# Feed-forward pairs of a two-block transformer layer: a pair's up result evacuated in two parts inside the next pair, one weight sum moved behind a plain unit, a group's last activation turned at once

## The chip, the cores and the metric

One Trainium2 chip, one core. The metric is the device time of one execution in microseconds. The kernel before took 2154.33 us (median of three runs, 2153.94 to 2155.76).

The engines are named as in the profile: PE (TensorE, matrix products; PEld is its loading of the stationary operand), DVE (VectorE), ACT (ScalarE), POOL (GpSimd) and SP (SyncE, which issues the large loads).

## The reference, cut to what matters

Two blocks run one after the other on 256 tokens of width 2048, in float32: an attention layer with four kinds of attention, and a mixer layer. The change touches only the feed-forward part of the second block:

```python
y = _rms(h, norm_ffn_g[i])                                   # 256 x 2048
h = h + (jax.nn.silu(y @ w_gate[i]) * (y @ w_up[i])) @ w_down[i]
```

`w_gate` and `w_up` are 2048 x 5632, `w_down` is 5632 x 2048.

## The kernel before, in words

**Products.** Every float32 operand is split into a rounded part `hi` and a remainder `lo`, and each product is made of three matmuls (x_hi w_lo, x_hi w_hi, x_lo w_hi). A weight tile of 512 rows by 512 columns (1 MB, `raw`) is loaded by SP, cast to `hi` by ACT (L292) and subtracted to `lo` by DVE (L293).

**Units.** The whole program is a list of units, each with one weight tile (`run_units`, L258). At step j the kernel issues, in this order: the sums that stand before unit j (`plus(u.before)`, L277, DVE), its hi (ACT), its lo (DVE), the sums behind it (`plus(u.after)`), then the products and evacuation of unit q = j - 2 (`fn`), then one step of the first waiting task (`pump`), then the loads whose buffer has come free (`fetch`). Three hi and lo buffers rotate, so hi of unit j needs PE to be done with unit j - 3. All engines work through their instructions in the order of issue.

**A plain unit** has 24 matmuls: four 128-row slices of the weight, two halves of the tokens, three matmuls each.

**Pairs.** The 5632 columns are taken in 11 blocks of 512, in groups of 4, 4 and 3. A block's gate and up tiles make a pair (`pair_units`, L304), but for the first block of all, which is computed plainly. For the first 1024 of the 2048 rows the pair takes the two halves of the tokens, two halves of the rows and the two weights as a 2 x 2 by 2 x 2 block product and makes it with seven products in place of eight, from sums of weight tiles and prepared sums of the activations (`forms`). Each of the seven is a form unit of 12 matmuls: u1, u5, u6, u3, u7, u4, u2. The other 1024 rows are plain units: left0 and left1 (the code's `left`, gate) and right0 and right1 (`right`, up). Four accumulators of PE are used: a and b end as gate, c and d as up. Their banks come in turn from five.

- u5 leaves its product in c, and ACT copies it to the tile `sn` (`keep`, L328, "s5"); u6 adds to b, and ACT keeps minus b in `sn` ("s2"); u7 adds to b, and ACT copies minus b into the bank of d (L353). Then left0 adds first to a (12 matmuls) and then to b (12 matmuls).
- The sums on weight tiles are b11 += b12 ahead of u5, b11 += b22 behind u5's lo, b12 += b22 ahead of u6, and b11 += b21 behind u7's lo. The last makes what u4 reads.
- u2 ends gate; ACT writes its Silu into two tiles `sg` (L1436).
- right1 ends up: `up_evac` (L1438) adds the kept `sn` to c and to d (L1446), then multiplies by the row scale and by `sg` into the tile `act` (L1449), all on DVE, and adds a task that turns `act` (`late_turn`, L393: four empty steps, one more in `turn_gen`, then eight transposes on PE, L431, and two copies each on ACT, L447, and DVE, L448, into `xB`).

**The order around the change** (`weave`, L382): the last two units of what came before, here called right0 and right1 of the previous pair, stand among the first units of the next:

```
right0(prev) u1 right1(prev) u5 u6 u3 u7 left0 u4 left1 u2 right0 u1(next) right1 ...
```

In groups 1 and 2 the two units ahead of the first pair are the last two of the down product before. Behind a group's last pair come the units of the down product (`down_evac`, L1456): four column tiles, each over all blocks of the group; the unit that reads block i calls `need(("act", g, i))`, which finishes that block's turn there and then if it isn't done.

Of the kernel before, what the change touches and what calls it, by code (L numbers as in the profile page):

```python
# [9 lines left out]
F32 = mybir.dt.float32  # L10
F32R = mybir.dt.float32r
AF = mybir.ActivationFunctionType
ALU = mybir.AluOpType
# [4 lines left out]
P = 128  # L18
# [6 lines left out]
CH = 512  # L25
# [133 lines left out]
class Kernel:  # L159
# [144 lines left out]
    def pair_units(self, wl, wr, lhs, forms, evac_l, evac_r, need=None):  # L304

        nc = self.nc  # L310
        src = lambda w, r: w[r].rearrange("p (k n) -> p k n", n=CH)
        st = {}
        b11, b12, b21, b22 = (Load(src(w, r), 4, CH) for r in range(2) for w in (wl, wr))

        def product(key, x, hi, lo, first):
            xh, xl = x
            for k in range(4):
                for i, (x_, w_) in enumerate(((xh, lo), (xh, hi), (xl, hi))):
                    nc.tensor.matmul(  # L319
                        st[key], x_[:, k, :], w_[:, k, :], start=first and k + i == 0, stop=k == 3 and i == 2, skip_group_check=True  # L320
                    )

        def bank(key):
            st[key] = self.psM.tile([P, CH], F32, tag="mm", name="mm")

        def keep(key, src, scale):
            st[key] = self.p5.tile([P, CH], F32, tag="sn", name="sn", bufs=2)
            nc.scalar.activation(out=st[key], in_=st[src], func=AF.Copy, scale=scale)  # L328

        def block(r, m):  # L330
            return [x[:, 4 * r : 4 * r + 4, m * P : m * P + P] for x in lhs()]

        def p1(hi, lo):
            if need is not None:
                self.need(need)
            bank("a")
            bank("b")
            product("a", block(0, 0), hi, lo, True)
            nc.scalar.copy(out=st["b"], in_=st["a"])

        def p5(hi, lo):
            bank("c")
            product("c", forms()["F5"], hi, lo, True)
            keep("s5", "c", 1.0)

        def p6(hi, lo):
            product("b", forms()["F6"], hi, lo, False)
            keep("s2", "b", -1.0)

        def p7(hi, lo):  # L350
            product("b", forms()["F7"], hi, lo, False)
            bank("d")
            nc.scalar.activation(out=st["d"], in_=st["b"], func=AF.Copy, scale=-1.0)  # L353

        def p2(hi, lo):
            product("a", block(1, 0), hi, lo, False)
            evac_l((st["a"], st["b"]))

        def rest(w, r, keys, then=None):
            def fn(hi, lo):  # L360
                for m, key in enumerate(keys):
                    product(key, block(r, m), hi, lo, False)
                if then is not None:
                    then()

            return Unit(src(w, r), 4, CH, fn)

        form = lambda load, fn: Unit(None, 4, CH, fn, load)
        u1 = form(b11, p1)
        u5, u6, u3, u7 = form(b11, p5), form(b11, p6), form(b22, lambda hi, lo: product("c", forms()["F3"], hi, lo, False)), form(b12, p7)  # L370
        u4 = form(b11, lambda hi, lo: product("b", block(1, 1), hi, lo, False))
        u2 = form(b21, p2)
        left = [rest(wl, r, "ab") for r in (2, 3)]
        right = [rest(wr, 2, "cd"), rest(wr, 3, "cd", lambda: evac_r(st["c"], st["d"], st["s2"], st["s5"]))]
        u1.loads = [b11]
        u5.before, u5.loads = [(b11, b12)], [b12]
        u5.after, u5.loads = [(b11, b22)], [b12, b22]
        u6.before = [(b12, b22)]
        u7.after, u7.loads = [(b11, b21)], [b21]
        return [u1, u5, u6, u3, u7, left[0], u4, left[1], u2], right  # L380

    def weave(self, pairs):  # L382

        tail = [self.units.pop() for _ in range(2)][::-1]
        for head, right in pairs:
            u5 = head[1]
            tail[1].before, u5.before = u5.before, []
            tail[1].loads, u5.loads = tail[1].loads + u5.loads[:1], u5.loads[1:]
            self.units += [tail[0], head[0], tail[1]] + head[1:]
            tail = right  # L390
        self.units += tail

    def late_turn(self, *args):  # L393
        for _ in range(4):
            yield
        yield from self.turn_gen(*args)

    def forms_of(self, lhs, out):

        nc = self.nc  # L400
        hi, lo = lhs
        f = self.p5.tile([P, 4, 2, 4, P], F32R, tag="forms", name="forms")
        for n, key in enumerate(("F5", "F6", "F3", "F7")):
            out[key] = (f[:, n, 0], f[:, n, 1])
        for k in (0, 2):
            x = []
            for r in range(2):
                t = self.p5.tile([P, CH], F32, tag="sg", name="fx", bufs=2).rearrange("p (k t) -> p k t", k=2)
                ks = slice(4 * r + k, 4 * r + k + 2)
                nc.vector.tensor_tensor(out=t, in0=hi[:, ks, :].bitcast(F32), in1=lo[:, ks, :].bitcast(F32), op=ALU.add)  # L410
                x.append(t)
            s = [self.p5.tile([P, CH], F32, tag="sn", name="fs", bufs=2).rearrange("p (f k t) -> p f k t", f=2, k=2) for _ in range(2)]
            s5, s6, s3, s7 = s[0][:, 0], s[0][:, 1], s[1][:, 0], s[1][:, 1]
            a11, a21, a12, a22 = x[0][:, :, 0:P], x[0][:, :, P:T], x[1][:, :, 0:P], x[1][:, :, P:T]
            sub = lambda o, p, q: nc.vector.tensor_tensor(out=o, in0=p, in1=q, op=ALU.subtract)
            sub(s5, a21, a22)
            sub(s7, a11, a21)
            sub(s6, s5, a11)
            nc.vector.tensor_tensor(out=s3, in0=s6, in1=a12, op=ALU.add)
            for src, key in ((s5, "F5"), (s7, "F7"), (s6, "F6"), (s3, "F3")):  # L420
                h, l = (y[:, k : k + 2, :] for y in out[key])
                nc.scalar.copy(out=h, in_=src)
                nc.vector.tensor_tensor(out=l, in0=src, in1=h.bitcast(F32), op=ALU.subtract)
            yield
# [1001 lines left out]
    def ffn_units(self):  # L1426
        nc, a = self.nc, self.a
        kx = [(k, k) for k in range(KD)]
        wg, wu, wd = a["t_w_gate_2"], a["t_w_up_2"], a["t_w_down_2"]
        r3 = lambda m: self.rs[:, 6 + m : 7 + m]  # L1430
        sg, forms = {}, {}
# [3 lines left out]
                s = sg[m] = self.p5.tile([P, CH], F32, tag="sg", name="sg", bufs=2)  # L1435
                nc.scalar.activation(out=s, in_=ps[m], func=AF.Silu, scale=r3(m))  # L1436

        def up_evac(g, i):  # L1438
            def evac(*ps):
                t = self.p5.tile([P, 2, CH], F32, tag="act", name="act", bufs=1)  # L1440
                if len(ps) == 1:
                    ps = ps[0]
                else:
                    *ps, s2, s5 = ps
                    for m, s in enumerate((s2, s5)):
                        nc.vector.tensor_tensor(out=s, in0=ps[m], in1=s, op=ALU.add)  # L1446
                    ps = s2, s5
                for m in range(2):
                    nc.vector.scalar_tensor_tensor(out=t[:, m, :], in0=ps[m], scalar=r3(m), in1=sg[m], op0=ALU.mult, op1=ALU.mult)  # L1449
                if i == 0:  # L1450
                    self.actT = self.new_B()
                self.add(self.late_turn(lambda m: t[:, m, :], 4 * i, lambda: self.actT), name=("act", g, i))

            return evac

        def down_evac(g, c):  # L1456
            def evac(ps):
# [18 lines left out]
        for g, n in enumerate((4, 4, 3)):  # L1476
            lhs, pairs = lambda: self.yT2, []
            for i in range(n):
                if g == 0 and i == 0:
                    def fresh():  # L1480
                        self.to_ffn()
                        self.add(self.forms_of(self.yT2, forms), name="forms")

                    self.wide = [self.gemm(wg[0], kx, lhs, gate_evac, fresh=fresh, need=lambda gi: ("h2", gi))[0]]
                    self.gemm(wu[0], kx, lhs, up_evac(0, 0))
                else:
                    need = "forms" if g == 0 and i == 1 else None
                    pairs.append(self.pair_units(wg[c0 + i], wu[c0 + i], lhs, lambda: forms, gate_evac, up_evac(g, i), need))
            self.weave(pairs)
            kts = [(c0 * 4 + k, k) for k in range(4 * n)]  # L1490
            for c in range(4):
                tail = g == 2 and c == 0
                us = self.gemm(wd[c], kts, lambda: self.actT, down_evac(g, c), fresh=self.to_tail if tail else None, need=lambda gi, g=g: ("act", g, gi))
                if tail:
                    self.wide.append(us[0])
            c0 += n
# [116 lines left out]
```

## Time and profile before

| | us |
|---|---|
| median of three runs | 2154.33 |
| the profiled execution | 2153.68 |
| its span, first to last instruction | 2151.9 |
| PE busy | 2100.4 |
| DVE busy | 1325.9 |
| ACT busy | 989.8 |

The feed-forward stage runs from about 1310 to 2060 us of the span. The mean granted clock of PE over the span is 0.994 of full speed. A row of the trace gives its start and its length in us; "x2" joins neighbours of one kind; a bracket at the end is the engine's idle time ahead of the row and what is taken to have ended it. Where an instruction waits for several things, the profile names the one that came last by its record.

### The profile page before, as it was taken

Reading aid. Unit: us, or ns where it says so; the run is one execution under the profiler, and the core shown is the slowest. Engines: PE = TensorE matmul, PEld = TensorE weight load, DVE = VectorE, ACT = ScalarE, POOL = GpSimd, SP = SyncE. Lnnn points to the kernel's source line nnn. Section 1 sums busy time; section 2 is a strip of 40 time slices with the busy share of each in tenths; the row PEclk is TensorE's granted clock in tenths of the full one; section 3 lists DMA queues with packets and bytes.
Section 4 is the critical chain, followed back from the end, with each engine's and each line's share of the span. In section 5 each row is a group of like instructions: output and inputs, shape, how many; then the busy total and the mean of one; then the engine's idle time right before and its main releaser. Section 6 shows DMA issues by size and latency. Waiting matters only on the chain.

```text
span 2151.9 us, 22847 instructions
## 1 busy us (share of the span) xinstructions
PE 2100.4 (98%) x9472; PEld 1727.2 (80%) x9472; DVE 1325.9 (62%) x1110; ACT 989.8 (46%) x932; POOL 36.9 (2%) x65
## 2 busy tenths in 40 slices
PE   8999999999999999999999999999999999999998
PEld 6888888888888888888888888777877778777886
DVE  6457555544455555556599458874588744885554
ACT  5444444444344434445453545553355533554544
POOL 1100000000000000001000000000000000000000
PEclk9999999999999999999999999999999999999999
DMA  7744354455555555555655455555445554445453
GB/s 261 258 154 176 132 182 159 174 196 182 192 194 195 182 191 194 187 223 197 234 176 177 175 176 208 206 195 185 164 158 206 203 196 169 164 184 193 166 176 127
DMA packets 59128, 401.68 MB, mean 187 GB/s; under 512 B 6788, under 2 KB 7440, under 8 KB 12304
## 3 DMA queue, kind: packets, MB, share of 16 engines
q1 hardware_dynamic: 56592, 388.69, 50.3%
q0 software_dynamic: 2288, 11.43, 1.7%
q8 instruction: 74, 1.21, 0.2%
q14 instruction: 30, 0.25, 0.0%
q10 hardware_dynamic: 144, 0.11, 0.0%
HBM read 398.08 MB, written 4.47 MB: 187 GB/s over the span
## 4 chain that ended last, share of the span: by engine, by line
PE 87%; DVE 9%; issue 2%; ACT 1%; DMA 1%; SPq 0%; ACTq 0%; POOLq 0%; POOL 0%; DVEq 0%
PE mm L233 24%; PE mm L235 24%; PE mm L234 24%; PE mm L319 11%; DVE lo L293 5%; DVE raw L277 2%; PE at L431 2%; ACT hi L292 1%; DMA raw<-in_t_w_in_dram 1%; PE at L646 0%; DVE sn L1446 0%; PE at L988 0%; DVE act L1449 0%; PE at L638 0%; PE at L682 0%
## 5 line engine op out<-in xcount | busy, mean ns | idle before, releaser
L293 DVE TENSOR_TENSOR lo<-raw,hi 128x2048 fp32r<-128x2048 f32 (+3 forms) x405 | 906.6, 2247 | 608.8 <-ACT hi L292 608.6
L292 ACT CAST hi<-raw 128x2048 fp32r<-128x2048 f32 (+3 forms) x405 | 756.4, 1873 | 663.2 <-PE mm L235 473.8
L233 PE MATMUL mm<-lo,xA 128*128 128x512 f32 x1536 | 606.9, 395 | 7.1 <-DVE lo L293 6.2
L235 PE MATMUL mm<-hi,xA 128*128 128x512 f32 x1536 | 600.6, 391 | 0.0
L234 PE MATMUL mm<-hi,xA 128*128 128x512 f32 x1536 | 600.4, 391 | 0.0
L233 PEld LDWEIGHTS mm<-lo,xA 128*128 128x128 f32 x1536 | 289.8, 189 | 69.2 <-DVE lo L293 7.1
L235 PEld LDWEIGHTS mm<-hi,xA 128*128 128x128 f32 x1536 | 289.9, 189 | 61.1
L234 PEld LDWEIGHTS mm<-hi,xA 128*128 128x128 f32 x1536 | 290.0, 189 | 59.4
L319 PE MATMUL mm<-hi,xA 128*128 128x512 f32 x880 | 271.3, 389 | 0.0
L233 PE MATMUL mm<-lo,xB 128*128 128x512 f32 x608 | 242.7, 399 | 4.8 <-ACT xB L447 4.8
L235 PE MATMUL mm<-hi,xB 128*128 128x512 f32 x608 | 240.6, 396 | 5.1 <-DVE xB L448 5.1
L234 PE MATMUL mm<-hi,xB 128*128 128x512 f32 x608 | 239.5, 394 | 0.0
L319 PEld LDWEIGHTS mm<-hi,xA 128*128 128x128 f32 x880 | 165.2, 188 | 33.9
L319 PE MATMUL mm<-lo,xA 128*128 128x512 f32 x440 | 173.0, 393 | 7.0 <-DVE lo L293 7.0
L235 PEld LDWEIGHTS mm<-hi,xB 128*128 128x128 f32 x608 | 115.6, 190 | 32.9 <-DVE xB L448 6.4
L233 PEld LDWEIGHTS mm<-lo,xB 128*128 128x128 f32 x608 | 115.7, 190 | 29.7 <-ACT xB L447 5.5
L234 PEld LDWEIGHTS mm<-hi,xB 128*128 128x128 f32 x608 | 115.7, 190 | 24.5
L319 PEld LDWEIGHTS mm<-lo,xA 128*128 128x128 f32 x440 | 82.6, 188 | 28.0 <-DVE lo L293 11.3
L319 PE MATMUL mm<-hi,forms 128*128 128x512 f32 x320 | 100.4, 395 | 0.0
L277 DVE TENSOR_TENSOR raw<-raw 128x2048 f32<-128x2048 f32 x40 | 90.7, 2288 | 0.7
L319 PE MATMUL mm<-lo,forms 128*128 128x512 f32 x160 | 65.0, 406 | 15.0 <-ACT sn L328 12.3
L319 PEld LDWEIGHTS mm<-hi,forms 128*128 128x128 f32 x320 | 60.3, 189 | 13.3
(282 smaller groups left out, 1178.1 us busy)
## 6 DMA issues: line engine op xcount, KB each, us to landing
raw<-in_t_w_in_dram SPq DMA_DIRECT2D x164, 1024.0 KB, 4.8
raw<-in_t_w_gate_dram SPq DMA_DIRECT2D x44, 1024.0 KB, 4.8
raw<-in_t_w_up_dram SPq DMA_DIRECT2D x44, 1024.0 KB, 5.1
raw<-in_t_w_down_dram SPq DMA_DIRECT2D x44, 1024.0 KB, 4.8
raw<-in_t_w_out_dram SPq DMA_DIRECT2D x32, 1024.0 KB, 4.8
raw<-in_t_w_branch_dram SPq DMA_DIRECT2D x16, 1024.0 KB, 4.8
raw<-in_t_w_ple_gate_dram SPq DMA_DIRECT2D x16, 1024.0 KB, 4.8
raw<-in_t_w_in_dram SPq DMA_DIRECT2D x6, 512.0 KB, 7.7
```

What stands on the lines that cost most here:

```text
L233: nc.tensor.matmul(ps, xh[:, k, ts], lo, start=first, stop=False)
L234: nc.tensor.matmul(ps, xh[:, k, ts], hi, start=False, stop=False)
L235: nc.tensor.matmul(ps, xl[:, k, ts], hi, start=False, stop=last)
L277: nc.vector.tensor_tensor(out=x.flat(), in0=x.flat(), in1=y.flat(), op=ALU.add)
L292: nc.scalar.copy(out=hi[:, o], in_=vv[:, o])
L293: nc.vector.tensor_tensor(out=lo[:, o], in0=vv[:, o], in1=hi[:, o].bitcast(F32), op=ALU.subtract)
L319: nc.tensor.matmul(st[key], x_[:, k, :], w_[:, k, :], start=first and k + i == 0, stop=k == 3 and i == 2, skip_group_check=True)
L431: self.nc.tensor.transpose(out, in_, self.ident[: in_.shape[0], : in_.shape[0]])
```

## The change

1. `evac_r` is no longer called whole behind right1. It comes in two parts: the add and the product for c (part 0) behind u3 of the next pair, the same for d (part 1) behind u7 of the next pair. The last pair of a group does both parts behind its own right1, as before. The kept tiles `sn` get four buffers in place of two.
2. The product is written into `sg` itself; the tile `act` is gone. The transposes read `sg`.
3. The sum b11 += b21 and the load of b21 move from u7 to left0: the sum comes behind left0's lo.
4. `late_turn` has two empty steps in place of four, counted from part 1. For a group's last block `late_turn` is left out: `turn_gen` alone, so that the transposes come behind the first unit of the down product.

```diff
         def keep(key, src, scale):
-            st[key] = self.p5.tile([P, CH], F32, tag="sn", name="sn", bufs=2)
+            st[key] = self.p5.tile([P, CH], F32, tag="sn", name="sn", bufs=4)
...
-        right = [rest(wr, 2, "cd"), rest(wr, 3, "cd", lambda: evac_r(st["c"], st["d"], st["s2"], st["s5"]))]
+        right = [rest(wr, 2, "cd"), rest(wr, 3, "cd")]
+        ends = [lambda: evac_r(0, st["c"], st["s2"]), lambda: evac_r(1, st["d"], st["s5"])]
...
-        u7.after, u7.loads = [(b11, b21)], [b21]
-        return [u1, u5, u6, u3, u7, left[0], u4, left[1], u2], right
+        left[0].after = [(b11, b21)]
+        left[0].loads = left[0].loads + [b21]
+        return [u1, u5, u6, u3, u7, left[0], u4, left[1], u2], right, ends
...
-        tail = [self.units.pop() for _ in range(2)][::-1]
-        for head, right in pairs:
+        tail, ends = [self.units.pop() for _ in range(2)][::-1], ()
+        for head, right, after in pairs:
...
             self.units += [tail[0], head[0], tail[1]] + head[1:]
-            tail = right
+            for u, f in zip(head[3:5], ends):
+                then(u, f)
+            tail, ends = right, after
         self.units += tail
+        for f in ends:
+            then(tail[1], f)
 
     def late_turn(self, *args):
-        for _ in range(4):
+        for _ in range(2):
             yield
...
-        def up_evac(g, i):
...
+        def up_evac(g, i, late):
+            def part(m, ps, plus=None):
+                s = sg[m]
+                if plus is not None:
+                    nc.vector.tensor_tensor(out=plus, in0=ps, in1=plus, op=ALU.add)
+                    ps = plus
+                nc.vector.scalar_tensor_tensor(out=s, in0=ps, scalar=r3(m), in1=s, op0=ALU.mult, op1=ALU.mult)
+                if m == 1:
+                    t = [sg[0], sg[1]]
+                    if i == 0:
+                        self.actT = self.new_B()
+                    gen = self.late_turn if late else self.turn_gen
+                    self.add(gen(lambda m: t[m], 4 * i, lambda: self.actT), name=("act", g, i))
...
-                    pairs.append(self.pair_units(wg[c0 + i], wu[c0 + i], lhs, lambda: forms, gate_evac, up_evac(g, i), need))
+                    pairs.append(self.pair_units(wg[c0 + i], wu[c0 + i], lhs, lambda: forms, gate_evac, up_evac(g, i, i < n - 1), need))
```

`then(u, f)` calls f behind the products of unit u. The plainly computed first block calls both parts together, where it was evacuated before.

## Rows read from the trace of the kernel before

**Rows 1.** The page, part 1: busy time, share of the span, instructions of PE.

```profile
PE 2100.4 (98%) x9472; PEld 1727.2 (80%) x9472; DVE 1325.9 (62%) x1110; ACT 989.8 (46%) x932; POOL 36.9 (2%) x65
```

**Rows 2.** Waits of PE, 1300 to 2000 us: total us, times, longest us.

```profile
PE mm L319 <- ACT sn L328: 12.3, 7, 1.8
PE mm L319 <- DVE lo L293: 8.4, 13, 0.7
PE mm L235 <- DVE xB L448: 5.1, 3, 1.7
PE mm L233 <- ACT xB L447: 4.8, 3, 1.6
```

**Rows 3.** Timeline of PE in one pair: u6's end, u3, u7, left0.

```profile
1610.47 0.63 PE L319 MATMUL mm<-hi,forms 128*128 128x512 f32 x2
1612.85 0.47 PE L319 MATMUL mm<-lo,forms 128*128 128x512 f32 x1 [1.74 <-ACT sn L328]
...
1616.41 0.39 PE L319 MATMUL mm<-lo,forms 128*128 128x512 f32 x1
...
1617.81 0.39 PE L319 MATMUL mm<-lo,forms 128*128 128x512 f32 x1
...
1619.36 0.50 PE L319 MATMUL mm<-lo,xA 128*128 128x512 f32 x1 [0.69 <-DVE lo L293]
...
1621.54 0.39 PE L319 MATMUL mm<-lo,xA 128*128 128x512 f32 x1
...
1622.90 0.39 PE L319 MATMUL mm<-lo,xA 128*128 128x512 f32 x1
```

**Rows 4.** Timeline of DVE in the same pair.

```profile
1605.70 2.28 DVE L293 TENSOR_TENSOR lo<-raw,hi 128x2048 fp32r<-128x2048 f32 x1
1607.90 1.28 DVE L1446 TENSOR_TENSOR sn<-mm,sn 128x512 f32<-128x512 f32 x2
1609.10 1.40 DVE L1449 SCALAR_TENSOR_TENSOR act<-sn,rs,sg 128x512 f32<-128x512 f32 x2
1610.42 4.48 DVE L293 TENSOR_TENSOR lo<-raw,hi 128x2048 fp32r<-128x2048 f32 x2
1614.83 2.28 DVE L277 TENSOR_TENSOR raw<-raw 128x2048 f32<-128x2048 f32 x1
```

**Rows 5.** Timeline of ACT in the same pair.

```profile
1603.61 3.72 ACT L292 CAST hi<-raw 128x2048 fp32r<-128x2048 f32 x2 [3.30 <-DVE raw L277]
...
1612.22 0.60 ACT L328 ACTIVATE sn<-mm 128x512 f32<-128x512 f32 x1
...
1617.22 1.91 ACT L292 CAST hi<-raw 128x2048 fp32r<-128x2048 f32 x1 [2.60 <-DVE raw L277]
1619.03 0.57 ACT L353 ACTIVATE mm<-mm 128x512 f32<-128x512 f32 x1
```

**Rows 6.** Timeline of PE in group 1's first pair: u3.

```profile
1568.37 0.47 PE L319 MATMUL mm<-lo,forms 128*128 128x512 f32 x1 [0.43 <-DVE lo L293]
```

**Rows 7.** Timeline of PE where group 0's last block is turned.

```profile
1481.37 1.03 PE L431 MATMUL at<-ident,act 128*128 128x128 f32 x8
1484.00 0.50 PE L233 MATMUL mm<-lo,xB 128*128 128x512 f32 x1 [1.60 <-ACT xB L447]
...
1486.44 0.53 PE L235 MATMUL mm<-hi,xB 128*128 128x512 f32 x1 [1.71 <-DVE xB L448]
```

**Rows 8.** Stretches: length, busy by engine (PE, PEld, DVE, ACT, POOL), granted clock, DMA, GB/s.

```profile
1598.96:1644.34 45.38, 42.80 (x190) 34.41 (x189) 37.34 (x22) 24.87 (x19) 0.00 (x0) 1.00 0.51 186
1486.40:1490.00 3.60, 3.56 (x9) 2.84 (x10) 0.59 (x1) 0.00 (x0) 0.00 (x0) 0.55 0.81 289
1760.00:1763.00 3.00, 3.00 (x7) 2.42 (x8) 0.53 (x1) 0.00 (x0) 0.00 (x0) 0.50 0.88 287
1982.50:1989.00 6.50, 6.48 (x16) 5.12 (x17) 0.56 (x1) 0.00 (x0) 0.00 (x0) 0.54 0.44 161
```

**Rows 9.** The page, part 6: loads of the up weights, KB each, us to landing.

```profile
raw<-in_t_w_up_dram SPq DMA_DIRECT2D x44, 1024.0 KB, 5.1
```

More of the change, by code (lines that the diff above doesn't have):

```diff
@@ L378, in pair_units, with then, both @@
         u6.before = [(b12, b22)]
-        u7.after, u7.loads = [(b11, b21)], [b21]
-        return [u1, u5, u6, u3, u7, left[0], u4, left[1], u2], right
+        left[0].after = [(b11, b21)]
+        left[0].loads = left[0].loads + [b21]
+        return [u1, u5, u6, u3, u7, left[0], u4, left[1], u2], right, ends
     def weave(self, pairs):
-        tail = [self.units.pop() for _ in range(2)][::-1]
-        for head, right in pairs:
+        def then(u, f):
+            fn = u.fn
+            def both(hi, lo):
+                fn(hi, lo)
+                f()
+            u.fn = both
+        tail, ends = [self.units.pop() for _ in range(2)][::-1], ()
+        for head, right, after in pairs:
             u5 = head[1]
@@ L411, in forms_of @@
                 x.append(t)
-            s = [self.p5.tile([P, CH], F32, tag="sn", name="fs", bufs=2).rearrange("p (f k t) -> p f k t", f=2, k=2) for _ in range(2)]
+            s = [self.p5.tile([P, CH], F32, tag="sn", name="fs", bufs=4).rearrange("p (f k t) -> p f k t", f=2, k=2) for _ in range(2)]
             s5, s6, s3, s7 = s[0][:, 0], s[0][:, 1], s[1][:, 0], s[1][:, 1]
@@ L1436, in gate_evac, with both @@
                 nc.scalar.activation(out=s, in_=ps[m], func=AF.Silu, scale=r3(m))
-        def up_evac(g, i):
[L1439 to L1454, printed above, removed]
+        def up_evac(g, i, late):
[11 more added lines that the diff above has]
+                    self.add(gen(lambda m: t[m], 4 * i, lambda: self.actT), name=("act", g, i))
+            return part
+        def both(part):
+            return lambda ps: [part(m, ps[m]) for m in range(2)]
         def down_evac(g, c):
@@ L1484, in ffn_units @@
                     self.wide = [self.gemm(wg[0], kx, lhs, gate_evac, fresh=fresh, need=lambda gi: ("h2", gi))[0]]
-                    self.gemm(wu[0], kx, lhs, up_evac(0, 0))
+                    self.gemm(wu[0], kx, lhs, both(up_evac(0, 0, True)))
                 else:
                     need = "forms" if g == 0 and i == 1 else None
-                    pairs.append(self.pair_units(wg[c0 + i], wu[c0 + i], lhs, lambda: forms, gate_evac, up_evac(g, i), need))
+                    pairs.append(self.pair_units(wg[c0 + i], wu[c0 + i], lhs, lambda: forms, gate_evac, up_evac(g, i, i < n - 1), need))
             self.weave(pairs)
```

## The prediction

> **What bounds it now.** The page comes first: PE is busy 98% of the span [rows 1]. So a gain has to come out of PE's idle time, or out of stretches in which PE runs slowly. The waits view of the feed-forward stage names that idle time, 30.6 us in four groups [rows 2]: 12.3 us in seven waits on ACT's kept copies `sn`, 8.4 us in thirteen waits on DVE's `lo`, and 5.1 + 4.8 us in three waits each on the split activation `xB`. The change works on all four.
>
> An idle figure understates what a wait costs. A matmul row is 0.39 us long, but matmuls start 0.23 us apart (six of u7 in 1.40 us, six of left0 in 1.36 us [rows 3]), so 0.16 us of each wait lies under the last row; and the product after a wait is followed later than usual by about 0.1 us. I add 0.27 us per wait. In one pair (second of group 1) the two large waits then cost 1.74 + 0.27 = 2.0 us ahead of u3 and 0.69 + 0.27 = 1.0 us ahead of left0 [rows 3]: 3.0 us a pair. The small wait ahead of u6 stays.
>
> **Whose wait is it?** The row ahead of u3 names ACT `sn`. I read it otherwise. DVE worked without a hole from lo(u6) on: lo(u6), the four operations of evac_r to 1610.50, then lo(u3) from 1610.42, which lasts 2.28 us and ends at 1612.70; u3 starts at 1612.85 [rows 3, 4]. The second kept copy ends at 1612.82 [rows 5], but it reads bank b, and u3 writes bank c. So u3 waited for lo(u3), which stood behind evac_r's 1.28 + 1.40 us. left0 waited the same way: its lo stood behind the sum at 1614.83 [rows 4]. DVE is late from u6 to left0, where units of 2.8 us each ask for a lo of 2.28 us and some for a sum of 2.28 us too. Should PE after all wait for the kept copy, the sum below stays, because that copy is its first link.
>
> **The change, part by part.**
>
> *Evacuation in two parts.* Nothing is saved in DVE work: two adds and two products of 0.7 us each, as before. They move from between lo(u6) and lo(u3) to behind the sum in left0's step (part 0) and behind lo(u4) (part 1). hi(u3), the second of two casts from 1603.61, is done by 1607.33 [rows 5], so lo(u3) can start 2.5 us earlier, at 1607.9, and ends at about 1610.2, ahead of the start of u6's last product at 1610.70 [rows 3]: the 2.0 us go. Behind part 0 stand lo(u4), which hi(u4) holds longer (1.91 us against part 0's 1.35), and the copy into bank d (L353), which needs part 0's add. Behind part 1 stands lo(left1), which by the same lengths ends only some 0.2 us ahead of PE: if missed, it costs about that. Four `sn` buffers let the kept copies run as soon as their product is done; this alone would gain nothing if lo is what PE waits for.
>
> *The sum behind left0.* b11 += b21 moves from ahead of lo(left0) to behind it; lo(left0) gains 2.2 us and the 1.0 us ahead of left0 goes. But hi(u4) reads this sum, and ACT issues hi(u4) ahead of the copy of bank b into bank d (L353). left0 accumulates into bank a in its first half and into bank b in its second, and the second must wait until L353 has read b. Now L353 ends at 1619.60, while left0 started at 1619.36 and needs b 2.7 us later [rows 3, 5]: hidden. After the change the chain from the start of u6's last product is: the product 0.4, second kept copy 0.6, hi(left0) 1.9, lo(left0) 2.28, sum 2.28, hi(u4) 1.91, L353 0.57, which makes 9.94 us; overlaps of neighbours on one engine take 0.28 off and hand-overs (0.11 us from sum to hi [rows 4, 5]) add 0.2: 9.9 us. PE's work up to there is 0.23 + 2.79 (u3) + 2.79 (u7) + 2.72 (12 products of left0) = 8.5 us, by the spacings above. A **new wait of 1.4 us in the middle of left0**, 1.5 with the slow restart. No row of before shows it, so I bound it: if L353 waited only for part 0's add and not behind hi(u4), about 0.1 us; if part 0 ran ahead of the sum, 1.4 us more, 2.9 in all. The order of issue in the code gives 1.5, which I take.
>
> So each of the seven pairs that follow a pair in their group gains 3.0 - 1.5 = 1.5 us, 10.5 us in all. The three first pairs of a group have no two-part evacuation ahead of them: u3's wait (0.43 us in group 1 [rows 6]) stays, left0's goes, and the new wait is shorter by what u3 still waits, about 0.8 us: 0.2 us gained each in groups 1 and 2. In group 0 the first block's act is now turned behind u3 instead of behind left0, so that its eight transposes (a row of 1.03 us [rows 7], some 0.8 us ahead of the next product) fill what is left of the new wait: 1.0 us gained. Pairs together: **11.9 us**.
>
> *A group's last act turned at once.* Now the turn waits until the down unit that reads it needs it: transposes at 1481.37, then PE idles 1.60 us for ACT's `xB` and, two products on, 1.71 us for DVE's [rows 7], since hi and lo of a later unit stand ahead of them on both engines. With the turn behind the group's first down unit there are one or two plain units (24 products, 5.4 us each) in between. ACT's two copies and DVE's two, at 0.6 to 0.7 us as their other operations on 512 columns [rows 4, 5], fit beside a hi of 1.91 and a lo of 2.28 us. All 9.9 us go [rows 2], with 6 x 0.27 = 1.6 us. And there is a second cost: behind these waits the granted clock is 0.55, 0.50 and 0.54 over 3.6, 3.0 and 6.5 us [rows 8], at or near the lower of its two levels (0.50, 1.2 GHz), after two idle stretches within 5 us. Lost there: 3.6 x 0.45 + 3.0 x 0.50 + 6.5 x 0.46 = 6.1 us. Sum: **17.6 us**.
>
> *The rest, at nothing.* The turn of a pair moves two steps on, behind left1; transposes read `sg` directly, and the next Silu into it comes one unit (2.7 us) later. Its copies on ACT now stand ahead of the next hi(u1), which has u2 and a plain unit, over 8 us. The load of b21 moves behind left0's on SP's queue: issued one release later, needed one unit later, still seven units ahead, at 5.1 us to landing [rows 9]; no wait of PE in the stage names a load [rows 2]. POOL's queue is not passed.
>
> **Sum.** 11.9 + 17.6 = 29.5 us. The profiled execution took 2153.68 us (span 2151.9), 0.65 under the median 2154.33. 2153.68 - 29.5 = 2124.2; against the median 2124.8.
>
> **The rivals.**
> 1. *Only the group ends gain*: left0's wait comes out at 2.9 us and gives the pairs back what u3 and left0 saved. For it: lo(u4), sum and part 0 meet in one DVE queue. Against it: part 0 is issued behind the sum. 2154.3 - 17.6 = 2136.7 us.
> 2. *Only the pairs gain*: the early turn meets a queue of its own and PE waits one unit earlier, with the slow clock. Against it: a plain unit of 5.4 us asks ACT for 1.91 and DVE for 2.28 us. 2142.4 us.
> 3. *No new wait*: bank b is free in time. 7 x 1.4 + 2 x 0.7 = 11.2 us more gained, 2113.6 us. The order on ACT speaks against it.
> 4. *Slower*: the new wait in left0 halves the clock, as the waits for `xB` did. A product then takes 0.43 instead of 0.23 us (7 in 3.00 us [rows 8]). If it held to the end of u4, 24 products x 0.2 = 4.8 us in ten pairs: 2172.8 us. It decides against the change from (29.5 + 4.3) / 10 = 3.4 us a pair, 17 products. Against it: the pair of rows 3 idles 1.74 and 0.69 us within 7 us at a granted clock of 1.00 [rows 8], more than it will afterwards. The Trainium skill, "TensorE: Matmul & The Clock Gate" (A second HAM failure mode: psum-queue depth-cycling), says that PE pausing briefly but often between groups of matmuls makes the clock swing between its levels; by that rule it would be this rival's time. In the pairs the trace does not show it, at the group ends it does.
> 5. *It does not do what it says*: the waits only change places, 2154 us.
>
> **How the numbers follow.** Forecast 0.70; rival 1 0.10, rival 2 0.08, rival 3 0.06, rival 4 0.03, rival 5 0.03. Of a difference, about 0.2% (4.3 us) can be told from none; all but rivals 4 and 5 are faster by more: 0.94, 0.03, 0.03. The bounds of the new wait set the range: 0.1 us instead of 1.5 gives 2113, 2.9 us in the seven pairs gives 2134.6; with rival 1 it reaches 2137.
>
> **What would show it.** Right: no wait of u3 on `sn` and none of left0's first product on `lo` in pairs that follow a pair; a wait of about 1.4 us in the middle of left0, released by ACT's L353, ten or nine times; a distance between pairs of 43.9 us instead of 45.38; no PE wait on `xB`, and a granted clock of 1.00 behind each group. Wrong: a wait for `xB` one unit earlier, a granted clock under 1 in left0, u3 waiting still, or the `left0` wait missing.

## The result, and the profile after

| | before | changed |
|---|---|---|
| median, us | 2154.14 (four runs) | 2125.09 (four runs, 2122.77 to 2126.75) |
| ratio | | 0.9863, 95% interval 0.9846 to 0.988 |
| profiled execution, us | 2153.68 | 2126.75 |
| its span | 2151.9 | 2125.0 |

The forecast was 2124.8 us. The two profiled executions differ by 26.9 us of span. 2.0 us of the gain are hidden in them: from 36 to 42 us, long before any changed instruction, the granted clock was 0.72 in the execution of the kernel before and 0.50 in that of the changed one. From the first pair on the changed kernel gains 28.9 us.

The waits of PE from 1300 to 2000 us (total us, times, longest us) answer to [rows 2]:

```profile
PE mm L319 <- ACT mm L353: 9.4, 9, 1.2
PE mm L319 <- DVE lo L293: 1.4, 3, 0.6
```

30.6 us in 26 waits have become 10.8 in 12. No wait on `xB` and none on `sn` is left, and the only new name is L353, the copy of bank b into bank d. The timeline of PE in the pair of [rows 3] (start, length, engine, line) shows where:

```profile
1602.82 0.40 PE L319 MATMUL mm<-lo,forms 128*128 128x512 f32 x1
1603.05 0.64 PE L319 MATMUL mm<-hi,forms 128*128 128x512 f32 x2
1603.53 0.39 PE L319 MATMUL mm<-lo,forms 128*128 128x512 f32 x1
...
1609.10 0.40 PE L319 MATMUL mm<-lo,xA 128*128 128x512 f32 x1
...
1611.40 0.61 PE L319 MATMUL mm<-hi,xA 128*128 128x512 f32 x2
1613.20 0.50 PE L319 MATMUL mm<-lo,xA 128*128 128x512 f32 x1 [1.18 <-ACT mm L353]
```

u3 follows u6 at 1603.53 with no break, left0 follows u7 at 1609.10 with none, and in left0's middle, behind 12 products, PE idles 1.18 us; with the 0.27 us that an idle figure leaves out, 1.45. The reason stands in the timelines of DVE (first fence) and ACT (second):

```profile
1598.29 4.49 DVE L293 TENSOR_TENSOR lo<-raw,hi 128x2048 fp32r<-128x2048 f32 x2
1602.95 2.29 DVE L293 TENSOR_TENSOR lo<-raw,hi 128x2048 fp32r<-128x2048 f32 x1 [0.17 <-ACT hi L292]
1606.15 2.29 DVE L293 TENSOR_TENSOR lo<-raw,hi 128x2048 fp32r<-128x2048 f32 x1 [0.91 <-ACT hi L292]
1608.36 2.28 DVE L277 TENSOR_TENSOR raw<-raw 128x2048 f32<-128x2048 f32 x1
1610.56 0.69 DVE L1459 TENSOR_TENSOR sn<-mm,sn 128x512 f32<-128x512 f32 x1
```

```profile
1603.73 0.60 ACT L328 ACTIVATE sn<-mm 128x512 f32<-128x512 f32 x1 [0.81 <-PE mm L319]
1604.22 1.89 ACT L292 CAST hi<-raw 128x2048 fp32r<-128x2048 f32 x1
1610.75 1.91 ACT L292 CAST hi<-raw 128x2048 fp32r<-128x2048 f32 x1 [4.64 <-DVE raw L277]
1612.56 0.58 ACT L353 ACTIVATE mm<-mm 128x512 f32<-128x512 f32 x1
```

This is the chain of the forecast link by link: kept copy 1603.73, hi(left0) 1604.22, lo(left0) 1606.15, sum 1608.36, hi(u4) 1610.75, L353 1612.56 to 1613.14, second half of left0 at 1613.20. lo(u3), the second of the two from 1598.29, is done at 1602.8, before u6 ends.

Group 1's first pair, timeline of PE, answers to [rows 6]; u3's wait stays, left0's middle waits less than half as long:

```profile
1561.10 0.47 PE L319 MATMUL mm<-lo,forms 128*128 128x512 f32 x1 [0.43 <-DVE lo L293]
1570.17 0.50 PE L319 MATMUL mm<-lo,xA 128*128 128x512 f32 x1 [0.54 <-ACT mm L353]
```

Stretches, as in [rows 8] (length, busy by engine, granted clock, DMA, GB/s): one pair, then the units behind the three groups' turns.

```profile
1591.55:1635.47 43.92, 42.59 (x190) 34.46 (x189) 37.76 (x22) 24.98 (x19) 0.00 (x0) 1.00 0.52 190
1480.00:1487.00 7.00, 7.00 (x32) 5.77 (x31) 3.67 (x3) 2.79 (x2) 0.00 (x0) 1.00 0.53 179
1743.00:1750.00 7.00, 7.00 (x32) 5.73 (x31) 3.33 (x3) 2.26 (x2) 0.00 (x0) 1.00 0.55 171
1957.00:1966.00 9.00, 9.00 (x41) 7.39 (x40) 4.17 (x4) 4.16 (x6) 0.00 (x0) 1.00 0.60 207
```

A pair takes 43.92 instead of 45.38 us, and behind the groups PE is busy without a hole at a clock of 1.00.

**Where each part came from.** The table compares the profiled execution of each kernel with that of before at seven places of PE's order, by the start of the instruction with the same number: where the first pair begins (1324.51 us before), and for each group where the pairs end and where the down product has taken in the turn (1464.88 and 1499.60, 1738.42 and 1773.96, 1966.44 and 1996.38). For the changed kernel these are 1326.54; 1463.05 and 1492.33; 1726.58 and 1756.77; 1946.16 and 1969.45. Between one group's turn and the end of the next group's pairs lies unchanged work besides: the -1.0 of "four buffers alone" stands in the down product ahead of group 1's pairs, where 241 products of PE in place of 247 fall into 56 us at a clock of 1.00; why is not shown. Figures are us gained.

| kernel | median | pairs of group 0, 1, 2 | sum | ends of group 0, 1, 2 | sum |
|---|---|---|---|---|---|
| forecast | 2124.8 | 4.0, 4.7, 3.2 | 11.9 | 5.5, 5.4, 6.8 | 17.6 |
| changed | 2125.09 | 3.85, 4.57, 3.09 | 11.5 | 5.44, 5.35, 6.65 | 17.4 |
| turn at once alone | 2136.66 | 0, 0, 0 | 0 | 5.45, 5.37, 6.63 | 17.5 |
| last turn two steps late, alone | 2142.94 | 0, 0, 0 | 0 | 4.66, 4.57, 1.19 | 10.4 |
| four buffers alone | 2153.78 | 0, -1.0, 0 | -1.1 | -0.2, -0.9, 1.2 | 0.1 |
| sum moved alone | 2149.91 | 0.65, 0.87, 0.53 | 2.1 | 0.1, -0.1, 1.2 | 1.2 |
| two parts alone, late turn | 2126.11 | 5.37, 6.76, 4.51 | 16.6 | 4.66, 4.57, 2.77 | 12.0 |
| changed, last turn late | 2132.42 | 3.81, 4.58, 3.01 | 11.4 | 4.65, 4.58, -0.2 | 9.0 |
| changed, sum back | 2118.61 | 5.33, 6.77, 4.47 | 16.6 | 5.44, 5.35, 6.65 | 17.4 |
| changed, sum in halves | 2119.46 | 5.20, 7.27, 5.13 | 17.6 | 5.44, 5.35, 6.65 | 17.4 |
| changed, half the sum back | 2112.98 | 6.90, 9.84, 6.88 | 23.6 | 5.44, 5.35, 6.65 | 17.4 |
| changed, sum on POOL | 2158.38 | -6.10, -10.83, -6.23 | -23.2 | 5.45, 5.37, 6.63 | 17.5 |

The forecast's group figures are its pieces put together (group 0: 1.0 + 1.5 + 1.5; its end 1.60 + 1.71 + 0.54 + 3.6 x 0.45).

### The profile page after: what moved, and what is told of

Its sections match the earlier page's. It is cut to its first block, busy times and chain, and to the rows that moved or that the text cites. A ratio compares the mean times of both kernels' runs of the same rounds, so it can differ in the third digit from the quotient of the medians.

```text
span 2125.0 us, 22838 instructions
## 1 busy us (share of the span) xinstructions
PE 2092.6 (98%) x9472; PEld 1724.2 (81%) x9472; DVE 1330.1 (63%) x1110; ACT 991.0 (47%) x932; POOL 36.6 (2%) x65
## 3 DMA queue, kind: packets, MB, share of 16 engines
HBM read 398.08 MB, written 4.47 MB: 189 GB/s over the span
```

## The experiments

**One part alone: the last turn at once.**

```diff
...
-                self.add(self.late_turn(lambda m: t[:, m, :], 4 * i, lambda: self.actT), name=("act", g, i))
+                gen = self.late_turn if late else self.turn_gen
+                self.add(gen(lambda m: t[:, m, :], 4 * i, lambda: self.actT), name=("act", g, i))
...
-                    pairs.append(self.pair_units(wg[c0 + i], wu[c0 + i], lhs, lambda: forms, gate_evac, up_evac(g, i), need))
+                    pairs.append(self.pair_units(wg[c0 + i], wu[c0 + i], lhs, lambda: forms, gate_evac, up_evac(g, i, i < n - 1), need))
```

> The kernel before with one edit: a group's last block is turned at once. Theory (the group ends cost 17.6 us, 11.5 in waits and 6.1 in half-clocked products behind them): 2154.1 - 17.6 = 2136.5 us, no PE wait on xB, granted clock 1.00 behind all three groups, the pairs unchanged at 45.4 us apart. Rival (the low clock has another cause than these waits): the waits go but the clock stays low, 2142.6 us. Rival (only the pairs gained): 2154 us.

2136.66 us, ratio 0.9921 (0.9908 to 0.9935). PE's waits, 1300 to 2000 us:

```profile
PE mm L319 <- ACT sn L328: 12.3, 7, 1.8
PE mm L319 <- DVE lo L293: 8.4, 13, 0.7
```

The `xB` rows are gone, the pairs are as before, and the whole 17.5 us come, the clock's share among them: behind the three groups (1480 to 1492, 1743 to 1760, 1962 to 1975 us) the granted clock is 1.00.

**Is it the kept copy that u3 waits for?** Four `sn` buffers alone, with the product written into `sg`, which makes the room.

```diff
-            st[key] = self.p5.tile([P, CH], F32, tag="sn", name="sn", bufs=2)
+            st[key] = self.p5.tile([P, CH], F32, tag="sn", name="sn", bufs=4)
...
-                t = self.p5.tile([P, 2, CH], F32, tag="act", name="act", bufs=1)
...
-                    nc.vector.scalar_tensor_tensor(out=t[:, m, :], in0=ps[m], scalar=r3(m), in1=sg[m], op0=ALU.mult, op1=ALU.mult)
+                    nc.vector.scalar_tensor_tensor(out=sg[m], in0=ps[m], scalar=r3(m), in1=sg[m], op0=ALU.mult, op1=ALU.mult)
...
```

> The kernel before with four sn buffers and the product written into sg itself (which makes the room); evacuation, sum and turn stay where they were. Theory (u3 waits for its lo, which stands behind the evacuation on DVE): 2154 us within 1.5, the kept copies no longer wait, u3 still idles 1.7 us in seven pairs. Rival (the profile's row is right, u3 waits for the kept copy): the 2.0 us ahead of u3 go in seven pairs, 2140 us.

2153.78 us, ratio 1.0 (0.999 to 1.0009). PE's waits:

```profile
PE mm L319 <- DVE lo L293: 20.7, 20, 1.8
PE mm L235 <- DVE xB L448: 5.1, 3, 1.7
PE mm L233 <- ACT xB L447: 4.8, 3, 1.6
```

12.3 us on `sn` in seven waits and 8.4 on `lo` in thirteen have become 20.7 us on `lo` in twenty: the same waits, the same length, under their right name. With two buffers the second kept copy happened to end 0.1 us behind lo(u3), and the profile names what ends last. With four the copy is done at 1612.35, lo(u3) at 1613.31, and u3 starts behind the latter (the pair of [rows 3]; ACT, DVE, PE):

```profile
1611.75 0.60 ACT L328 ACTIVATE sn<-mm 128x512 f32<-128x512 f32 x1 [0.81 <-PE mm L319]
```

```profile
1611.03 2.28 DVE L293 TENSOR_TENSOR lo<-raw,hi 128x2048 fp32r<-128x2048 f32 x1
```

```profile
1613.46 0.47 PE L319 MATMUL mm<-lo,forms 128*128 128x512 f32 x1 [1.75 <-DVE lo L293]
```

**Two parts alone.** The changed kernel with two lines turned back:

```diff
...
-        left[0].after = [(b11, b21)]
-        left[0].loads = left[0].loads + [b21]
+        u7.after, u7.loads = [(b11, b21)], [b21]
...
-                    pairs.append(self.pair_units(wg[c0 + i], wu[c0 + i], lhs, lambda: forms, gate_evac, up_evac(g, i, i < n - 1), need))
+                    pairs.append(self.pair_units(wg[c0 + i], wu[c0 + i], lhs, lambda: forms, gate_evac, up_evac(g, i, True), need))
```

> The changed kernel with the sum b11 += b21 and its load back behind u7 and the last block turned late: of the change only the two-part evacuation is left. Theory: u3's 2.0 us go in seven pairs; left0's first product still waits for its lo, which stands behind the sum (about 0.8 us printed idle); no wait in the middle of left0, as hi(u4) has its sum early: 43.3 us from pair to pair, 15.6 us less with the earlier turn in group 0, 2138.5 us. That would be more than the pairs gained in the whole change (about 11.3 us): the sum's move would then cost some 4 us. Rival (the sum has to move too for the pairs to gain, as the stall goes over to left0 in full): 2150 us or more.

2126.11 us, ratio 0.9873 (0.9859 to 0.9886): 12 us under what was expected, and as fast as the whole change. PE's waits, then ACT's L353 in a pair of group 1:

```profile
PE mm L319 <- DVE lo L293: 5.8, 12, 0.7
PE mm L233 <- ACT xB L461: 2.1, 3, 1.6
PE mm L235 <- DVE xB L462: 1.7, 1, 1.7
```

```profile
1608.09 0.58 ACT L353 ACTIVATE mm<-mm 128x512 f32<-128x512 f32 x1 [0.88 <-DVE sn L1458]
```

The pairs gave 16.6 us (0.9 of it in group 0's first pair, by its earlier turn), about the 15.6 expected and 5 more than in the whole change. left0's own wait is 0.43 us idle and the middle of left0 has none: L353, done at 1608.67, now waits for part 0's add. The other 12 us were not expected: with the turn "late" as in the changed file, two of the three pairs of waits on `xB` are nearly gone all the same. What I had left out is that the change shortens `late_turn` too. The next two runs take that up.

**Two steps late, alone.** In the kernel before, only the last block's `late_turn` gets two empty steps in place of four.

```diff
...
-        for _ in range(4):
+        for _ in range(n):
...
-                self.add(self.late_turn(lambda m: t[:, m, :], 4 * i, lambda: self.actT), name=("act", g, i))
+                self.add(self.late_turn(lambda m: t[:, m, :], 4 * i, lambda: self.actT, n=4 if late else 2), name=("act", g, i))
...
```

> The kernel before with one edit: late_turn of a group's last block has two empty steps in place of four; all other turns as before. PE makes the transposes at the same place in groups 0 and 1, behind the third down unit, but from the pump, so ahead of the next hi and lo in the queues of ACT and DVE. Theory (the queue position is the cost): 5.4 - 0.8 us saved in each of groups 0 and 1, nothing in group 2: 2145 us. Rival (the distance between transposes and the unit that needs them is the cost): 2154 us.

2142.94 us, ratio 0.9953 (0.9938 to 0.9967). PE's waits on `xB`:

```profile
PE mm L233 <- ACT xB L447: 2.1, 3, 1.6
PE mm L235 <- DVE xB L448: 1.7, 1, 1.7
```

The transposes stand at the same place of PE's order in groups 0 and 1, behind the third down unit and before the fourth, which reads them. Only ACT and DVE have them ahead of the next hi and lo instead of behind. That alone takes 9.2 us (4.66 + 4.57). The 1.2 us of group 2 are a shorter low-clock stretch behind the same waits: 0.61 over 3.3 us (1972.7 to 1976) and 0.86 over the next 3.0, where [rows 8] has 0.54 over 6.5. Queue position, not distance, was the cost.

**The changed kernel with the last turn late.** One edit: `up_evac(g, i, True)`.

> The changed kernel with the last block of a group turned late, by the late_turn that the change has shortened to two empty steps. In groups 0 and 1 the transposes then come behind the third down unit, still one pump ahead of the need; in group 2, of three blocks, the need forces them. Theory (what costs is that a forced turn stands behind the next hi and lo in the queues of ACT and DVE): groups 0 and 1 lose 0.8 us each, group 2 3.8 us in waits and up to 3 us at the low clock, 2130 to 2134 us. Rival (only the turn at once saves the 17.6 us): 2142.7 us.

2132.42 us, ratio 0.9899 (0.9884 to 0.9914). So of the 17.4 us at the group ends the shortened `late_turn` would have brought 9.2; leaving it out brings the other 8: 0.8 us in each of groups 0 and 1 and all of group 2, where with three blocks the need comes a unit earlier.

**The sum moved, alone.** The kernel before with b11 += b21 and its load behind left0.

```diff
-        u7.after, u7.loads = [(b11, b21)], [b21]
+        left[0].after = [(b11, b21)]
+        left[0].loads = left[0].loads + [b21]
```

> The kernel before with only the sum b11 += b21 and its load moved behind left0. Theory: left0's first wait (0.69 us idle) goes, a wait of about 0.7 us for L353 in its middle comes, u3's 1.74 us stay: 0.2 us a pair, 2152 us. Rival (the move by itself is worth the whole 1.0 us a pair): 2144 us. Rival (the new wait is as long as in the changed kernel, 1.2 us, whatever stands ahead): 2158 us.

2149.91 us, ratio 0.9984 (0.9975 to 0.9993). From PE's waits:

```profile
PE mm L319 <- ACT sn L328: 12.3, 7, 1.8
...
PE mm L319 <- ACT mm L353: 4.8, 10, 0.6
```

The middle of left0 waits in all ten pairs, 0.48 us each, and u3 waits as before. The pairs gain 2.1 us; the rest of the median's gain lies within the interval and in the clock behind the groups.

**The sum back, all else changed.** The first edit of the run "two parts alone" (the sum back), without its second.

> The changed kernel with the sum b11 += b21 and its load back behind u7; the two-part evacuation and the turn at once stay. Theory (the sum's move costs more than it gains, as it puts the sum, hi(u4) and L353 in one chain): the wait in left0's middle (1.18 us idle) goes, one of 0.43 us ahead of left0 comes, as measured with the evacuation alone; 43.1 instead of 43.9 us from pair to pair, 2119.5 us. Rival (the pairs gain by the sum's move as the change has it): 2130 us or more, left0 idle 0.7 us or more.

2118.61 us beside 2125.35 for the changed kernel on the same chip. Of the 5.9 us between the two profiled spans 5.0 lie in the pairs and 0.8 ahead of the first pair, in unchanged work. PE's only waits in the stage:

```profile
PE mm L319 <- DVE lo L293: 5.8, 12, 0.7
```

**The changed kernel again**, for that comparison.

> The changed kernel once more, beside the next three on one chip: 2125 us within 1.5.

2125.35 us, ratio 0.987 (0.9853 to 0.9886).

**The moved sum in halves.** Is the chain sum, hi(u4), L353 what left0's middle waits for? Shorten it and see.

```diff
...
+        left[0].halves = True
+        u4.parts = [2, 2]
...
+                for k in range(0, 4, 2 if halves else 4):
+                    o = slice(k * CH, (k + (2 if halves else 4)) * CH)
+                    nc.vector.tensor_tensor(out=x.flat()[:, o], in0=x.flat()[:, o], in1=y.flat()[:, o], op=ALU.add)
...
```

> The changed kernel with the moved sum made as two operations of half the width and hi and lo of u4 in two halves each, so that the first half of hi(u4) runs beside the second of the sum. Theory (the middle of left0 waits for the chain sum, hi(u4), L353): the chain is 0.7 us shorter, the idle time falls from 1.18 to about 0.45 us in seven pairs, 2119 us. Rival (L353 waits for something else, part 0's add or the bank): the wait stays at 1.2 us, 2125 us or a little more for the added operations.

2119.46 us, ratio 0.9842 (0.9827 to 0.9856). PE's wait:

```profile
PE mm L321 <- ACT mm L355: 2.2, 7, 0.3
```

1.18 us idle have become 0.31: the chain it is.

**Half of the sum on either side of lo(left0).**

```diff
...
-        left[0].after = [(b11, b21)]
-        left[0].loads = left[0].loads + [b21]
+        u7.after, u7.loads = [(b11, b21, 0, 2)], [b21]
+        left[0].after = [(b11, b21, 2, 4)]
+        u4.parts = [2, 2]
...
+            for x, y, *part in pairs:
+                k0, k1 = part or (0, 4)
+                o = slice(k0 * CH, k1 * CH)
+                nc.vector.tensor_tensor(out=x.flat()[:, o], in0=x.flat()[:, o], in1=y.flat()[:, o], op=ALU.add)
...
```

> The changed kernel with half of the sum behind u7's lo, half behind left0's lo, and hi and lo of u4 in two halves. Theory: lo(left0) is late by only 1.1 us, for which there is room, and L353 ends ahead of left0's second half: neither wait, 42.5 us from pair to pair, 2113 us, under both kernels. Rival (DVE has no room for even half a sum ahead of lo(left0)): a wait of 0.4 us or more stays, 2117 us or more.

2112.98 us (2112.27 to 2113.29), ratio 0.9811 (0.9796 to 0.9826), under both kernels. PE's waits, then DVE in one pair:

```profile
PE mm L321 <- DVE lo L295: 1.4, 3, 0.5
```

```profile
1598.95 1.22 DVE L279 TENSOR_TENSOR raw<-raw 128x1024 f32<-128x1024 f32 x1
1600.09 2.28 DVE L295 TENSOR_TENSOR lo<-raw,hi 128x2048 fp32r<-128x2048 f32 x1
1602.29 1.22 DVE L279 TENSOR_TENSOR raw<-raw 128x1024 f32<-128x1024 f32 x1
1603.43 0.69 DVE L1462 TENSOR_TENSOR sn<-mm,sn 128x512 f32<-128x512 f32 x1
```

Both waits of left0 are gone. What is left in the row are the three first pairs' waits of u3.

**The sum on POOL.** If DVE's queue is what is short, take the sum off it.

```diff
...
-        left[0].after = [(b11, b21)]
-        left[0].loads = left[0].loads + [b21]
+        u6.loads, u6.pool = [b21], [(b11, b21)]
...
+                for x, y in u.pool:
+                    nc.gpsimd.tensor_tensor(out=x.flat(), in0=x.flat(), in1=y.flat(), op=ALU.add)
...
```

> The changed kernel with the sum b11 += b21 made by POOL behind u6's lo in place of DVE. Theory (DVE's queue is what is short from u6 to left0): with the sum off DVE both waits of left0 go if POOL needs less than some 9 us for it, 2113 us. No row shows how long POOL takes for 128x2048: at 9 us a wait of 0.4 us stays, 2117 us; every us more costs one in each of ten pairs, and from about 11 us on it is slower than the changed kernel. Rival (POOL's work slows DVE's beside it): lo rows of DVE longer than 2.3 us while POOL works.

2158.38 us, ratio 1.0019 (1.001 to 1.0029): slower than before. PE's waits; POOL's and DVE's timelines in one pair; then the stretches of PE's wait and behind it:

```profile
PE mm L321 <- DVE lo L293: 33.1, 10, 3.9
```

```profile
1613.73 6.58 POOL L297 TENSOR_TENSOR raw<-raw 128x2048 f32<-128x2048 f32 x1 [43.73 <-DVE lo L293]
```

```profile
1613.57 2.29 DVE L293 TENSOR_TENSOR lo<-raw,hi 128x2048 fp32r<-128x2048 f32 x1
1616.04 6.43 DVE L293 TENSOR_TENSOR lo<-raw,hi 128x2048 fp32r<-128x2048 f32 x1 [0.18 <-ACT hi L292]
```

```profile
1619.00:1622.60 3.60, 0.55 (x3) 0.13 (x2) 3.60 (x2) 2.10 (x2) 1.32 (x1) 1.00 0.29 123
1622.60:1626.00 3.40, 3.38 (x8) 2.72 (x9) 3.36 (x4) 0.00 (x0) 0.00 (x0) 0.50 0.66 234
```

The rival to this run's theory won. POOL needed 6.6 us at most, under the 9 that would have done; but lo(u7), which starts while POOL works, takes 6.43 us and ends 2.15 us behind POOL's end at 1620.31. PE stands for 3.0 to 3.9 us in each of the ten pairs, and behind eight of these waits, this one among them, the clock falls to 0.50.

## Why the prediction was right

*Whose wait.* Right: u3 waited for lo(u3) behind the evacuation on DVE; four buffers alone changed nothing.

*Two parts.* Right in what goes (u3's 2.0 us in seven pairs, none in the three first pairs), and lo(left1) behind part 1 was in time. But its worth was given away in part: without the sum's move the pairs gain 16.6 us.

*The sum behind left0.* The new wait was sized well: 1.18 us idle and 1.45 in all, against 1.4 of lateness and 1.5 in all, through the chain that was forecast, and in seven pairs in full, in two (first pairs of groups 1 and 2) in part, in group 0's first pair not at all. By the starts of the same product the pair of [rows 3] gains 1.99 us at u3 and 0.96 at left0 and loses 1.45 in left0's middle, so the 0.27 us added to each idle figure held too. The seven pairs gain 1.43 to 1.49 us each, against 1.5; the three first pairs 0.96, 0.15 and 0.17, against 1.0, 0.2 and 0.2. What I did not work out is the account of this part by itself. I booked left0's 1.0 us to it. Once lo(u3) and lo(u7) are in time, the sum ahead of lo(left0) costs only 0.43 + 0.27 = 0.7 us, so moving it buys 0.7 and costs 1.45. The move is a loss of 5 us in the changed kernel (16.6 against 11.5) and a gain of 2.1 only without the two parts. The forecast's total stands because it used both ends of the exchange as they are in the changed kernel.

*The turn at once.* Right in size, 17.4 against 17.6, and in the second cost: the low clock behind the waits went with them. The reason given, that a forced turn stands behind the next hi and lo, is what the runs show. Not seen: over half of it (9.2 us) would have come from the shorter `late_turn` alone.

*Nothing for the rest.* Right: no wait of PE names a load or the Silu into `sg`.

*Rivals.* Only the ends, or only the pairs: both fall by the table. No new wait: falls by L353's row. Slower by the clock in left0: the pair's stretch has a clock of 1.00; a wait of 1.2 us in mid-unit, 44 us apart, did not lower it. The rule of the Trainium skill named there, "TensorE: Matmul & The Clock Gate" (A second HAM failure mode: psum-queue depth-cycling), did not show in the pairs; at the group ends, where the prediction saw it, PE had two waits of 1.60 and 1.71 us ahead of the low clock, no frequent short ones. The waits only changing places falls by the time, 2125.09 us. The run with POOL shows the price of being wrong there: behind eight of its ten waits of 3.0 to 3.9 us the clock was 0.50.

## What to carry to other kernels

When one engine's queue is the shortage, ask of each moved operation what now stands behind it on its own engine and on the next: the sum freed lo(left0), but tied hi(u4) and an unrelated copy to itself, and cutting the operation in two around the urgent one beat both orders. A task forced by the instruction that needs it lands behind everything already issued on the other engines; issued one step earlier it costs nearly nothing, with PE's order unchanged. Price a wait by what follows it too: 11.5 us of waits at the group ends came with 6 us lost to products at half the clock.

## What the runs showed of the hardware that was not expected

- POOL and DVE exclude each other. A subtraction of DVE on two SBUF tensors took 6.43 us in place of 2.29 when POOL's addition of two SBUF tensors was under way at its start; it ended 2.15 us behind POOL's, so nearly its whole length lay behind it. One begun 0.16 us ahead of POOL's kept its 2.29 us, and there POOL's took longer: 6.53 to 6.59 us in these seven pairs, against 4.59 to 4.60 in the three first pairs. In those first pairs DVE was, at POOL's start, at two operations that each read one operand from an accumulator bank (`mm`; timelines of POOL and DVE in group 1's first pair below), and they kept their 0.7 us beside POOL's. The Trainium skill, "GPSIMD Engine Reference" (Specifications), says that POOL shares its SBUF interfaces with VectorE, with contention for DVE instructions with two SBUF inputs; these rows agree, and put a figure to it.

```profile
1565.42 4.59 POOL L297 TENSOR_TENSOR raw<-raw 128x2048 f32<-128x2048 f32 x1 [127.93 <-DVE lo L293]
```

```profile
1565.20 1.28 DVE L1480 TENSOR_TENSOR R<-R,mm 128x512 f32<-128x512 f32 x2
```

- The clock does not fall each time behind the same waits. Behind group 2's forced turn in the run "two parts alone", with the same 1.6 and 1.7 us of idle time, it stayed at full speed: that end gained 2.77 us on the kernel before, where the runs "changed, last turn late" and "two steps late", with the same waits and a low clock behind them, gained -0.2 and 1.19. The stretch, with the columns of the stretches above:

```profile
1957.00:1961.00 4.00, 4.00 (x18) 3.29 (x19) 0.53 (x1) 0.00 (x0) 0.00 (x0) 1.00 0.73 262
```

In the run with POOL the clock stayed at 1.00 behind two of the ten waits:

```profile
1439.80:1445.00 5.20, 5.20 (x23) 4.24 (x24) 5.17 (x4) 2.14 (x2) 0.00 (x0) 1.00 0.85 299
1900.40:1905.00 4.60, 4.60 (x20) 3.81 (x21) 4.56 (x4) 1.58 (x2) 0.00 (x0) 1.00 0.73 280
```

The twelve pairs of these `xB` waits in the profiled executions of all kernels were followed by a low clock eleven times, for shorter or longer. So the 6.1 us of the forecast is what the three cost in one execution, and no fixed price.
